# Crossing from one sub-layer to the next: where a row is normalised, who writes its high and low part, and where its transposes stand

## The chip, the cores and the metric

The kernel runs on one core of a Trainium2 chip. The metric is the device time of one launch in microseconds (us). Five engines work side by side, each through its own queue in order: TensorE (PE in the rows, PEld its weight loads), VectorE (DVE), ScalarE (ACT), GpSimd (POOL) and SyncE (SP), which issues most of the DMA transfers.

## The reference, cut to what matters

Two layers of a hybrid backbone over 256 latent and 256 context tokens with 1024 channels. A layer is three sub-layers: a SwiGLU FFN, a mixer of three branches, another FFN. Each takes a modulated input and is followed by a post-norm:

```python
def _ln(x):
    xf = x.astype(jnp.float32)
    mu = jnp.mean(xf, axis=-1, keepdims=True)
    var = jnp.mean(jnp.square(xf - mu), axis=-1, keepdims=True)
    return ((xf - mu) * lax.rsqrt(var + LN_EPS)).astype(x.dtype)

def _post_norm(x, res, g, b):
    return _ln(DN_ALPHA * x + res) * g + b

def _modulate(x, shift, scale):
    return _ln(x) * (1.0 + scale) + shift

# in a layer, for latent tokens (h) and context tokens (hc) alike:
h = _post_norm(h, 0.5 * m[2] * _swiglu(_modulate(h, m[0], m[1]), ...), ...)
y, yc = _mixer(_modulate(h, m[3], m[4]), _modulate(hc, mc[3], mc[4]), ...)
h = _post_norm(h, m[5] * y, ...)
h = _post_norm(h, 0.5 * m[8] * _swiglu(_modulate(h, m[6], m[7]), ...), ...)
```

Between two sub-layers stand two normalisations of the same row: the post-norm of the one and the modulation of the next.

## The kernel before

The 512 tokens are four token tiles of 128 rows (`h`, tokens on partitions); after the second layer's mixer only the two latent tiles go on. Every float32 operand of a matrix product is kept as a high and a low part (type fp32r), and a product is three matmuls, `mm3` (L73): high by high, high by low, low by high. Weights come in chunks (`chunk`, L57): a DMA brings `raw`, ScalarE casts the high part `whi` (L68), VectorE subtracts for the low part `wlo` (L69).

The last step of each sub-layer is a product `pd` with tokens on partitions, tile after tile: in an FFN 11 steps of three matmuls for each half of the columns, 33 products of 512 columns a tile in the last half, in a mixer 24 for each half. When a tile's half is done, `evac` takes it from PSUM into `h` on VectorE (`ev` L259, `h` L262 or L264) and collects statistics (`bst`, `bn` L190). After the second half `boundary` (L268) does the post-norm: aggregate `mv` (L202), the reciprocal root by `nv` on VectorE (L196) and a power on GpSimd (L197), `xn1` on VectorE (L275, the rows show it as `xn`), `h` with its row sum `q` (L276, L280), the sum of squares on ScalarE (L281), and again `nv` and the power. `normed` (L205) multiplies mean and root (`nb`, L210, VectorE) and lets ScalarE write the normalised row `xn` (L211). `modulate` (L214) transposes `xn` on TensorE in eight blocks of 128 x 128 into two PSUM tiles `put` (L222), ScalarE writes the scaled and shifted blocks `uv` (L231), VectorE casts them to the high part `uhi` (L233), and GpSimd subtracts for the low part `ulo` (L234). `uhi` and `ulo` are what the next sub-layer multiplies: its first products are `pg` and `pu` in an FFN (three matmuls each, high by high first) and `pgm` in a mixer.

There are five such seams: FFN to mixer, mixer to FFN, FFN to FFN of the next layer, FFN to mixer, each with four tiles, and mixer to FFN with two. The order of each engine's instructions is made by a scheduler from priorities that follow the order in the program. Tiles 0 and 1 have their `boundary` directly behind their own `evac`. For tiles 2 and 3 it is written after `mark`, and the first products of the next sub-layer, which need only tiles 0 and 1, are put ahead of these by `early`.

Of the kernel before, what the change touches and what calls it, by code (L numbers as in the profile page):

```python
# [8 lines left out]
F32 = mybir.dt.float32  # L9
# [5 lines left out]
D = 1024  # L15
# [11 lines left out]
class Kernel:  # L27
    def __init__(self, tc, ctx, I, out):
# [7 lines left out]
        self.dram = P(name="dram", bufs=1, space=bass.MemoryType.DRAM)  # L36

    def early(self):
        """Ahead of the boundary work of the context tokens."""
        return self.tc.high_priority(offset=self.tc.cur_priority - self.mark)  # L40
# [10 lines left out]
    def side(self, shape, name):  # L51
        """A PSUM tile for work between the matrix products."""
        pool, tag = self.spare
        return pool.tile(shape, F32, name=name, tag=tag)

    # ---------------------------------------------------------------- weights
    def chunk(self, ap, n=2048, pool=None, bufs=None):  # L57
        """[128, n] float32 in DRAM -> list of ([128, 1024] high part, low part)."""
# [14 lines left out]
    def mm3(self, ps, a, b, start, stop):  # L73
        """ps += a^T b, with a, b (high, low) pairs."""
# [30 lines left out]
    def mod_first(self, j, pool):  # L105
        """Shift and scale of model channels 128 j .. 128 j + 127 in the first sub-layer."""
# [22 lines left out]
    def modulate_first(self, j, pool, xn):  # L129
        """u of model channels 128 j .. 128 j + 127, all tokens."""  # L130
# [12 lines left out]
    def mod_out(self, l, n, res):  # L143
        """Adds the bias to columns 512 n .. 512 n + 511; gates go to DRAM as rows."""
# [19 lines left out]
    def mod(self, l, n):  # L164
        """Columns 512 n .. 512 n + 511 of both streams' modulation vectors of layer l, 128 (on partitions) a step."""
# [26 lines left out]
    def rsqrt(self, var, scale):  # L192
        """(var * scale + eps) ** -0.5"""
# [11 lines left out]
    def normed(self, pool, tt, nmu, rs, bufs=2):  # L205
        """(h + nmu) rs of one token tile."""
# [7 lines left out]
    def modulate(self, pool, l, slot, tt, xn, gs=(0, 1), dve=0):  # L214
        """u (feature-major, high and low) = xn (1 + scale) + shift for one token tile."""
        nc = self.nc
        s = TT_S[tt]
        cs = slice(128 * tt, 128 * tt + 128)
        for g in gs:
            pt = self.psd.tile([128, 4, 128], F32, name="put", tag="d")  # L220
            for j in range(4):
                nc.tensor.transpose(pt[:, j], xn[:, 128 * (4 * g + j):128 * (4 * g + j) + 128], self.ident)  # L222
# [1119 lines left out]
```

## Time and profile before

| | before |
|---|---|
| median of 3 runs | 2058.04 us |
| lowest and highest | 2054.61 and 2058.64 us |
| span of the profiled execution | 2059.9 us |
| TensorE busy | 1980.4 us, 96% |
| VectorE busy | 1519.5 us, 74% |
| ScalarE busy | 781.1 us, 38% |
| GpSimd busy | 157.0 us, 8% |

The span is that of one execution, taken with the profiler on. Busy times are sums over it. A matmul's row starts when it enters the array and lasts longer than the distance to the next one, since they are pipelined; how fast they go is read from the distance of two starts. The number in brackets behind a row is how long the engine stood idle before it, and what ended that.

### The profile page before, as it was taken

The numbers are of one execution on the slowest core, as the hardware profiler recorded it, in microseconds if no ns is written. First come the engines' busy times: TensorE is split into PE (matmuls) and PEld (weight loads), VectorE is DVE, ScalarE is ACT, GpSimd is POOL, SyncE is SP. The second block draws the span as 40 slices with busy tenths as digits, with TensorE's granted clock in tenths as the row PEclk, the third lists the DMA queues.
The fourth block names the chain that finished last, engine by engine and source line by source line (L and its number), as shares of the span: only waits on it lengthen the run. The fifth ranks groups of instructions, "written<-read, shape, count | busy, mean of one in ns | idle before, by whom it ended". The sixth has DMA issues, their size and how long they took to land. (4 is left out here: it accounts for less than half of the span.)

```text
span 2059.9 us, 28737 instructions
## 1 busy us (share of the span) xinstructions
PE 1980.4 (96%) x10556; PEld 1644.6 (80%) x10556; DVE 1519.5 (74%) x3352; ACT 781.1 (38%) x1300; POOL 157.0 (8%) x221
## 2 busy tenths in 40 slices
PE   7999999999999999999999989999998999979997
PEld 4888887787767887888888878888887877968896
DVE  4996998868996347766998767768778587684555
ACT  4321332345554224432233252312224566444442
POOL 0000110121100002200000030000003110010000
PEclk9999999999999999999999999999999999998999
DMA  8454566355344333345565525546552643564563
GB/s 312 154 152 143 184 202 215 118 178 163 120 147 133 101 103 123 113 148 180 184 197 186 187 97 188 166 158 198 173 183 88 188 156 117 163 232 136 182 188 112
DMA packets 103119, 333.10 MB, mean 162 GB/s; under 512 B 12353, under 2 KB 25505, under 8 KB 102977
## 3 DMA queue, kind: packets, MB, share of 16 engines
q1 hardware_dynamic: 96384, 310.96, 47.6%
q10 hardware_dynamic: 3584, 14.24, 1.8%
q0 software_dynamic: 3008, 6.07, 1.0%
q8 instruction: 83, 1.36, 0.3%
q14 instruction: 60, 0.48, 0.1%
HBM read 313.70 MB, written 17.51 MB: 161 GB/s over the span
## 5 line engine op out<-in xcount | busy, mean ns | idle before, releaser
L68 ACT CAST whi<-raw 128x1024 fp32r<-128x1024 f32 (+1 forms) x384 | 394.9, 1031 | 615.6 <-PE pd L78 160.2
L69 DVE TENSOR_TENSOR wlo<-raw,whi 128x1024 fp32r<-128x1024 f32 (+1 forms) x384 | 462.7, 1207 | 219.8 <-ACT whi L68 218.3
L178 DVE SCALAR_TENSOR_TENSOR pj<-raw,cb 128x512 f32<-128x512 f32 x512 | 351.7, 706 | 51.3 <-DMA raw<-in_w_modT 47.7
L76 PE MATMUL pg<-uhi,whi 128*128 128x512 f32 (+1 forms) x736 | 265.7, 361 | 1.6 <-DVE uhi L233 1.3
L78 PE MATMUL pg<-uhi,wlo 128*128 128x512 f32 (+1 forms) x736 | 263.1, 357 | 2.3 <-DVE wlo L69 2.3
L76 PE MATMUL pu<-uhi,whi 128*128 128x512 f32 (+1 forms) x736 | 263.2, 358 | 1.5 <-DVE ev L259 1.5
L77 PE MATMUL pg<-ulo,whi 128*128 128x512 f32 (+1 forms) x736 | 263.2, 358 | 0.6 <-POOL ulo L234 0.5
L77 PE MATMUL pu<-ulo,whi 128*128 128x512 f32 (+1 forms) x736 | 262.7, 357 | 0.0
L78 PE MATMUL pu<-uhi,wlo 128*128 128x512 f32 (+1 forms) x736 | 262.5, 357 | 0.0
L77 PE MATMUL pd<-wlo,gT 128*128 128x512 f32 x616 | 240.6, 391 | 1.6 <-DVE wlo L69 1.5
L76 PE MATMUL pd<-whi,gT 128*128 128x512 f32 x616 | 240.8, 391 | 0.9 <-DVE ev L259 0.9
L78 PE MATMUL pd<-whi,gT 128*128 128x512 f32 x616 | 239.5, 390 | 0.0
L76 PEld LDWEIGHTS pg<-uhi,whi 128*128 128x128 f32 x736 | 140.9, 191 | 26.1 <-issue 3.8
L78 PEld LDWEIGHTS pg<-uhi,wlo 128*128 128x128 f32 x736 | 140.7, 191 | 22.0 <-DVE wlo L69 2.7
L76 PEld LDWEIGHTS pu<-uhi,whi 128*128 128x128 f32 x736 | 140.9, 192 | 21.6 <-DVE ev L259 1.7
L77 PEld LDWEIGHTS pg<-ulo,whi 128*128 128x128 f32 x736 | 140.4, 191 | 20.9 <-POOL ulo L234 1.1
L77 PEld LDWEIGHTS pu<-ulo,whi 128*128 128x128 f32 x736 | 140.6, 191 | 20.2 <-issue 0.8
L78 PEld LDWEIGHTS pu<-uhi,wlo 128*128 128x128 f32 x736 | 140.5, 191 | 19.8 <-issue 0.4
L76 PEld LDWEIGHTS pd<-whi,gT 128*128 128x128 f32 x616 | 115.6, 188 | 27.2 <-issue 1.3
L77 PEld LDWEIGHTS pd<-wlo,gT 128*128 128x128 f32 x616 | 115.7, 188 | 25.9 <-DVE wlo L69 2.5
L78 PEld LDWEIGHTS pd<-whi,gT 128*128 128x128 f32 x616 | 115.7, 188 | 23.9
L76 PE MATMUL pgg<-uhi,whi 128*128 128x512 f32 (+1 forms) x384 | 131.8, 344 | 0.0
(561 smaller groups left out, 3234.0 us busy)
## 6 DMA issues: line engine op xcount, KB each, us to landing
raw<-in_w_gu SPq DMA_DIRECT2D x176, 512.0 KB
raw<-in_w_modT SPq DMA_DIRECT2D x128, 512.0 KB
raw<-in_w_dn SPq DMA_DIRECT2D x80, 512.0 KB
raw<-in_w_in SPq DMA_DIRECT2D x80, 512.0 KB
sd<-sst ACTq DMA_DIRECT2D x16, 802.0 KB
sst<-sd SPq DMA_DIRECT2D x16, 802.0 KB
wm<-in_w_mod SPq DMA_DIRECT2D x16, 512.0 KB
raw<-in_w_br SPq DMA_DIRECT2D x16, 512.0 KB
```

What stands on the lines that cost most here:

```text
L68: nc.scalar.copy(hi[:, :m], raw[:, :m])
L69: nc.vector.tensor_sub(lo[:, :m], raw[:, :m], hi[:, :m].bitcast(F32))
L76: mm(ps, a[0], b[0], start=start, stop=False)
L77: mm(ps, a[0], b[1], start=False, stop=False)
L78: mm(ps, a[1], b[0], start=False, stop=stop)
L178: V.scalar_tensor_tensor(junk, raw[:, 512 * k:512 * k + 512], 1.0, self.cb[:, s, 512 * k:512 * k + 512], op0=OP.mult, op1=OP.mult, accum_o ...
```

## The change

`normed`, `modulate`, `early` and `mark` are gone. In their place stands `feed`. It normalises the row on VectorE in one step, (h + nmu) * rs, with no `nb`; after the transposes, ScalarE writes each block's high part `uhi` straight from PSUM, VectorE computes the same block once more from PSUM in float32 (`uv`, eight operations of 128 columns), and VectorE, not GpSimd, subtracts for `ulo`.

`boundary` no longer calls this at once. It leaves it with `later(9.6, ...)`: `mm3` counts down the time of the products that are written after it, and when 9.6 us of them have been written, `feed` is written at that place. The transposes may not be issued ahead of the last matmul written by then (`issue_after`). `flush` writes at once what is left over: after the first half of the first `pg` and `pu` of an FFN, after the first pair of tiles of a mixer, and at the start of an FFN of two tiles. The last `evac`, `boundary` and `feed` are `urgent`, with a raised priority, for all tiles alike. `room` says from which pool and tags `xn` and `uv` take their buffers; in the mixer `uv` takes those of tag "p" (three), which `zs`, the copy that is stored for the state-space branch, uses too. The rest of the diff removes comments.

```diff
     def mm3(self, ps, a, b, start, stop):
         mm = self.nc.tensor.matmul
         mm(ps, a[0], b[0], start=start, stop=False)
         mm(ps, a[0], b[1], start=False, stop=False)
-        mm(ps, a[1], b[0], start=False, stop=stop)
+        self.last = mm(ps, a[1], b[0], start=False, stop=stop)
+        if self.todo:
+            us = 3 * (ps.free_size() + 32) / 2400
+            for x in self.todo:
+                x[0] -= us
+            while self.todo and self.todo[0][0] <= 0:
+                self.todo.pop(0)[1]()
...
+    def urgent(self):
+        return self.tc.high_priority(offset=400)
+    def later(self, us, step):
+        self.todo.append([us, step])
+    def flush(self):
+        todo, self.todo = self.todo, []
+        for _, step in todo:
+            step()
...
-        nc.vector.tensor_mul(nb, nmu, rs)
-        nc.scalar.activation(xn, self.h[:, tt], AF.Identity, bias=nb, scale=rs)
...
-                    nc.scalar.activation(v[:, j], pt[:, j], AF.Identity, bias=sh, scale=sc)
-            ks = slice(4 * g, 4 * g + 4)
-            nc.vector.tensor_copy(self.uhi[:, ks, cs], v)
-            (nc.vector if dve else nc.gpsimd).tensor_sub(self.ulo[:, ks, cs], v, self.uhi[:, ks, cs].bitcast(F32))
+    def feed(self, l, slot, tt, nmu, rs):
+        nc, V = self.nc, self.nc.vector
+        s = TT_S[tt]
+        cs = slice(128 * tt, 128 * tt + 128)
+        pool, xtag, vtag, pp, ptag = self.room
+        with self.urgent():
+            xn = pool.tile([128, D], F32, name="xn", tag=xtag[0], bufs=xtag[1])
+            V.tensor_scalar(xn, self.h[:, tt], nmu, rs, op0=OP.add, op1=OP.mult)
+            for g in range(2):
+                pt = pp.tile([128, 4, 128], F32, name="put", tag=ptag)
+                with self.tc.issue_after(self.last.ins):
+                    for j in range(4):
+                        nc.tensor.transpose(pt[:, j], xn[:, 128 * (4 * g + j):128 * (4 * g + j) + 128], self.ident)
+                v = pool.tile([128, 4, 128], F32, name="uv", tag=vtag[0], bufs=vtag[1])
+                for j in range(4):
+                    k = 4 * g + j
+                    sh = self.modT[l][:, 8 * slot + k, s:s + 1]
+                    sc = self.modT[l][:, 8 * slot + 8 + k, s:s + 1]
+                    nc.scalar.activation(self.uhi[:, k, cs], pt[:, j], AF.Identity, bias=sh, scale=sc)
+                    V.tensor_scalar(v[:, j], pt[:, j], sc, sh, op0=OP.mult, op1=OP.add)
+                ks = slice(4 * g, 4 * g + 4)
+                V.tensor_sub(self.ulo[:, ks, cs], v, self.uhi[:, ks, cs].bitcast(F32))
...
-        self.modulate(pool, *nxt, tt, self.normed(pool, tt, q[:, 1:2], self.rsqrt(q[:, 2:3], 1.0 / D)))
+        rs = self.rsqrt(q[:, 2:3], 1.0 / D)
+        self.later(9.6, lambda: self.feed(*nxt, tt, q[:, 1:2], rs))
...
+            self.room = pool, ("gT", 11), ("sg", 2), self.psd, "d"
+            if len(tiles) < 4:
+                self.flush()
...
-                        with self.early():
-                            W, begun = self.gate_load(l, f, range(2))
-                            self.gate_mm(W, begun, 0, T // 2)
+                        W, begun = self.gate_load(l, f, range(2))
+                        self.gate_mm(W, begun, 0, T // 2)
+                        self.flush()
                         self.gate_mm(W, begun, T // 2, T)
...
+                    self.room = bp, ("xn", 2), ("uv", 2), self.psd, "d"
                     for t in tiles:
                         for k in range(11):
                             step(k, t)
-                        self.evac(pool, nrm, t, ch, ps[t], False, True)
-                        if t < 2:
+                        with self.urgent():
+                            self.evac(pool, nrm, t, ch, ps[t], False, True)
                             self.boundary(bp, nrm, t, nxt)
-                    self.mark = tc.cur_priority
-                    for t in tiles[2:]:
-                        self.boundary(bp, nrm, t, nxt)
...
-                    with self.early():
-                        for _ in moving(ws, (store_z, store_v(0)), (0,)):
-                            pass
+                    self.room = pool, ("PT", 2), ("p", 3), self.psa, "a"
+                    for _ in moving(ws, (store_z, store_v(0)), (0,)):
+                        pass
+                    self.flush()
```

How this moves instructions is seen at the third seam, from the first layer's second FFN (`pd`) to the second layer's first (`pg`, `pu`). On TensorE, before, where `pd` ends:

```order
L78 MATMUL pd<-whi,gT 128x512
L76 MATMUL pg<-uhi,whi 128x256
L77 MATMUL pg<-ulo,whi 128x256
L222 MATMUL put<-ident,xn 128x128 x3
L78 MATMUL pg<-uhi,wlo 128x256
L222 MATMUL put<-ident,xn 128x128
L76 MATMUL pu<-uhi,whi 128x256
L77 MATMUL pu<-ulo,whi 128x256
L78 MATMUL pu<-uhi,wlo 128x256
L76 MATMUL pg<-uhi,whi 128x256
```

After, at the same place:

```order
L89 MATMUL pd<-whi,gT 128x512
L244 MATMUL put<-ident,xn 128x128 x8
L87 MATMUL pd<-whi,gT 128x512
L88 MATMUL pd<-wlo,gT 128x512
L89 MATMUL pd<-whi,gT 128x512
L87 MATMUL pg<-uhi,whi 128x256
L87 MATMUL pu<-uhi,whi 128x256
L87 MATMUL pg<-uhi,whi 128x256
L87 MATMUL pu<-uhi,whi 128x256
L88 MATMUL pg<-ulo,whi 128x256
L89 MATMUL pg<-uhi,wlo 128x256
L88 MATMUL pu<-ulo,whi 128x256
```

Before, the third tile's transposes stood between the first products of the next FFN; now those of the second tile stand three products ahead of the end of `pd`, and high-by-high products come first, then those with `ulo`.

On VectorE at this seam, before, from the aggregate of the third tile on:

```order
L202 BN_AGGR mv<-bst 128x2
L233 CAST uhi<-uv 128x4x128
L196 TENSOR_SCALAR nv<-mv 128x1
L275 SCALAR_TENSOR_TENSOR xn_10494<-h,mv,lng 128x1024
L233 CAST uhi<-uv 128x4x128
L276 SCALAR_TENSOR_TENSOR h,q<-xn_10494,nv,lnb 128x1024
L280 TENSOR_SCALAR q<-q 128x1
L69 TENSOR_TENSOR wlo<-raw,whi 128x1024
L196 TENSOR_SCALAR nv<-q 128x1
L210 TENSOR_TENSOR nb<-q,nv 128x1
L69 TENSOR_TENSOR wlo<-raw,whi 128x1024
L259 TENSOR_TENSOR ev<-pd,gbc_8531 128x512
```

After, from the evacuation of the fourth tile (`ev`) up to the second tile's first `ulo`:

```order
L278 TENSOR_TENSOR ev<-pd,gbc_8563 128x512
L80 TENSOR_TENSOR wlo<-raw,whi 128x1024
L213 TENSOR_SCALAR nv<-q 128x1
L251 TENSOR_SCALAR uv<-put,modT 128x128 x2
L283 TENSOR_TENSOR h<-h,ev 128x512
L251 TENSOR_SCALAR uv<-put,modT 128x128 x2
L207 BN_STATS bst<-h 128x6
L251 TENSOR_SCALAR uv<-put,modT 128x128
L219 BN_AGGR mv<-bst 128x2
L251 TENSOR_SCALAR uv<-put,modT 128x128
L253 TENSOR_TENSOR ulo<-uv,uhi 128x4x128
```

Before, VectorE did two casts per tile for the next sub-layer; now the second tile's eight `uv` stand one by one among the weights' `wlo` and the evacuation of the fourth, and the first `ulo` that the next products need stands behind all of them.

On VectorE at the fifth seam, from mixer to FFN with two tiles, before, from the second tile's last evacuation on:

```order
L259 TENSOR_TENSOR ev<-pd,gbc_16206 128x512
L262 SCALAR_TENSOR_TENSOR h<-h,ev 128x512
L190 BN_STATS bst<-h 128x6
L233 CAST uhi<-uv 128x4x128
L202 BN_AGGR mv<-bst 128x2
L196 TENSOR_SCALAR nv<-mv 128x1
L275 SCALAR_TENSOR_TENSOR xn_16431<-h,mv,lng 128x1024
L233 CAST uhi<-uv 128x4x128
L276 SCALAR_TENSOR_TENSOR h,q<-xn_16431,nv,lnb 128x1024
```

After, from the addition that follows it on:

```order
L281 SCALAR_TENSOR_TENSOR h<-h,ev 128x512
L251 TENSOR_SCALAR uv<-put,modT 128x128
L207 BN_STATS bst<-h 128x6
L251 TENSOR_SCALAR uv<-put,modT 128x128
L219 BN_AGGR mv<-bst 128x2
L251 TENSOR_SCALAR uv<-put,modT 128x128
L213 TENSOR_SCALAR nv<-mv 128x1
L294 SCALAR_TENSOR_TENSOR xn_16499<-h,mv,lng 128x1024
L251 TENSOR_SCALAR uv<-put,modT 128x128
L295 SCALAR_TENSOR_TENSOR h,q<-xn_16499,nv,lnb 128x1024
L251 TENSOR_SCALAR uv<-put,modT 128x128
L299 TENSOR_SCALAR q<-q 128x1
```

Before, two casts of the first tile stood in the chain of the second; now six of the first tile's `uv` do.

## Rows read from the trace of the kernel before

**Rows 1.** The page's part 1: busy time, share of the span, instructions.
```profile
PE 1980.4 (96%) x10556; PEld 1644.6 (80%) x10556; DVE 1519.5 (74%) x3352; ACT 781.1 (38%) x1300; POOL 157.0 (8%) x221
```

**Rows 2.** TensorE's waits: who for whom, us in total, times, longest.
```profile
PE put L222 <- ACT xn L211: 37.8, 18, 10.9
```

**Rows 3.** The five seams' windows: length, busy us by engine, clock, DMA.
```profile
390.00:440.00 50.00, 42.70 (x256) 38.00 (x255) 33.67 (x59) 26.15 (x50) 21.03 (x24) 0.93 0.23 72
795.00:845.00 50.00, 44.47 (x253) 38.73 (x252) 29.43 (x57) 25.19 (x49) 19.87 (x17) 0.97 0.16 48
1180.00:1230.00 50.00, 42.18 (x239) 36.93 (x238) 35.21 (x58) 25.43 (x48) 19.00 (x16) 0.93 0.24 87
1557.00:1607.00 50.00, 42.90 (x259) 37.98 (x258) 32.90 (x56) 25.87 (x49) 20.48 (x24) 0.97 0.33 105
1836.00:1866.00 30.00, 16.50 (x80) 13.90 (x79) 17.96 (x28) 13.81 (x26) 10.06 (x8) 0.72 0.38 130
```

**Rows 4.** TensorE's timeline, first seam: start, us, what, in brackets idle.
```profile
395.06 0.39 PE L78 MATMUL pd<-whi,gT 128*128 128x512 f32 x1
395.28 0.39 PE L76 MATMUL pd<-whi,gT 128*128 128x512 f32 x1
397.02 1.09 PE L222 MATMUL put<-ident,xn 128*128 128x128 f32 x8 [1.35 <-ACT xn L211]
...
418.88 1.76 PE L222 MATMUL put<-ident,xn 128*128 128x128 f32 x7 [4.05 <-ACT xn L211]
```

**Rows 5.** Timeline of the other engines, first seam, its first tile.
```profile
387.71 0.67 DVE L259 TENSOR_TENSOR ev<-pd,gbc 128x512 f32<-128x512 f32 x1
...
390.12 0.15 DVE L196 TENSOR_SCALAR nv<-mv 128x1 f32<-128x1 f32 x1
390.19 1.27 DVE L275 SCALAR_TENSOR_TENSOR xn<-h,mv,lng 128x1024 f32<-128x1024 f32 x1
...
390.36 1.53 POOL L197 TENSOR_TENSOR nv<-nv,mhalf 128x1 f32<-128x1 f32 x1 [44.26 <-DVE nv L196]
...
391.92 1.28 DVE L276 SCALAR_TENSOR_TENSOR h<-xn,nv,lnb 128x1024 f32<-128x1024 f32 x1 [0.46 <-POOL nv L197]
...
393.44 1.15 ACT L281 ACTIVATE xn<-h,q 128x1024 f32<-128x1024 f32 x1 [14.34 <-DVE q L280]
...
395.73 1.24 ACT L211 ACTIVATE xn<-h,nb,nv 128x1024 f32<-128x1024 f32 x1 [1.04 <-DVE nb L210]
```

**Rows 6.** TensorE's timeline: second seam's last tile, third seam's third.
```profile
836.37 1.09 PE L222 MATMUL put<-ident,xn 128*128 128x128 f32 x8 [2.12 <-ACT xn L211]
...
1210.60 0.90 PE L222 MATMUL put<-ident,xn 128*128 128x128 f32 x3 [4.14 <-ACT xn L211]
```

**Rows 7.** Timeline of GpSimd and VectorE, first seam, second and third tile.
```profile
412.23 1.29 POOL L234 TENSOR_TENSOR ulo<-uv,uhi 128x512 fp32r<-128x512 f32 x1
412.29 2.31 DVE L276 SCALAR_TENSOR_TENSOR h<-xn,nv,lnb 128x1024 f32<-128x1024 f32 x1 [0.45 <-POOL nv L197]
```

**Rows 8.** Timeline of TensorE, fifth seam: the second tile's transposes.
```profile
1856.97 1.97 PE L222 MATMUL put<-ident,xn 128*128 128x128 f32 x8 [10.92 <-ACT xn L211]
```

**Rows 9.** Groups by line and shape on VectorE and ScalarE: busy us, mean ns.
```profile
L69 DVE TENSOR_TENSOR wlo<-raw,whi 128x1024 fp32r<-128x1024 f32 x368 | 451.9, 1229 | 214.1 <-ACT whi L68 212.6 <-DMA mt<-kd 0.4
...
L233 DVE CAST uhi<-uv 128x512 fp32r<-128x512 f32 x36 | 20.4, 566 | 36.6 <-ACT uv L231 36.6
...
L141 DVE TENSOR_TENSOR ulo<-uv,uhi 128x512 fp32r<-128x512 f32 x8 | 5.5, 692 | 0.2
...
L633 DVE TENSOR_SCALAR sprm<-sprm,nsg 128x128 f32<-128x128 f32 x16 | 4.6, 285 | 4.6 <-DMA sprm<-in_ssm_bc 4.6
...
L157 DVE TENSOR_SCALAR grw<-pgt 8x128 f32<-8x128 f32 x12 | 3.3, 274 | 7.2 <-PE pgt L155 7.2
...
L781 DVE TENSOR_SCALAR ga<-ga 64x1024 f32<-64x1024 f32 x2 | 1.4, 676 | 0.0
...
L231 ACT ACTIVATE uv<-put,modT 128x128 f32<-128x128 f32 x144 | 52.5, 465 | 19.9 <-PE put L222 19.9
```

More of the change, by code (lines that the diff above doesn't have):

```diff
@@ L36, in __init__ @@
         self.dram = P(name="dram", bufs=1, space=bass.MemoryType.DRAM)
-    def early(self):
-        return self.tc.high_priority(offset=self.tc.cur_priority - self.mark)
+        self.todo = []
+    def urgent(self):
[6 more added lines that the diff above has]
+            step()
     def pool(self, es, name, side="left"):
@@ L212, in normed @@
         return xn
-    def modulate(self, pool, l, slot, tt, xn, gs=(0, 1), dve=0):
-        nc = self.nc
+    def feed(self, l, slot, tt, nmu, rs):
+        nc, V = self.nc, self.nc.vector
         s = TT_S[tt]
         cs = slice(128 * tt, 128 * tt + 128)
[L219 to L222, printed above, removed]
-            v = pool.tile([128, 4, 128], F32, name="uv", tag="uv", bufs=2)
-            for j in range(4):
-                k = 4 * g + j
-                sh = self.modT[l][:, 8 * slot + k, s:s + 1]
-                sc = self.modT[l][:, 8 * slot + 8 + k, s:s + 1]
-                if dve and j >= 4 - dve:
-                    nc.vector.tensor_scalar(v[:, j], pt[:, j], sc, sh, op0=OP.mult, op1=OP.add)
-                else:
-                    nc.scalar.activation(v[:, j], pt[:, j], AF.Identity, bias=sh, scale=sc)
-            ks = slice(4 * g, 4 * g + 4)
-            nc.vector.tensor_copy(self.uhi[:, ks, cs], v)
-            (nc.vector if dve else nc.gpsimd).tensor_sub(self.ulo[:, ks, cs], v, self.uhi[:, ks, cs].bitcast(F32))
@@ L1101, in mixer @@
                     self.psum(e2, d=3, o=2)
+                    self.room = pool, ("xn", 2), ("uv", 2), self.psd, "d"
                     w = [[x for i in range(2) for x in self.chunk(I["w_out"][l, ch, i], 2048, *((pool, 4) if ch else ()))] for ch in range(2)]
@@ L1111, in mixer @@
                                          (hi[:, o:o + 512], lo[:, o:o + 512]), start=k == 0, stop=k == 7)
-                            self.evac(pool, nrm, t, ch, ps, True, True)
-                        if t < 2:
+                            with self.urgent():
+                                self.evac(pool, nrm, t, ch, ps, True, True)
+                        with self.urgent():
                             self.boundary(pool, nrm, t, nxt)
-                    self.mark = self.tc.cur_priority
-                    for t in tiles[2:]:
-                        self.boundary(pool, nrm, t, nxt)
     def merge(self, l, pool, ys, yT, T, stationary, mo, ths):
```

## The prediction

> **What bounds the kernel now.** TensorE: the page has it busy for 96% of the span, VectorE for 74% [rows 1]. What TensorE can still win lies where it stands, so the list of its waits comes next: the transposes `put` wait for ScalarE's normalised row `xn`, 37.8 us in 18 waits, one for each token tile that crosses one of the five seams [rows 2]. The windows give each seam its idle time (length less PE busy) and the mean granted clock [rows 3]: 7.3, 5.5, 7.8, 7.1 and 13.5 us idle, in order; and the clock, 0.93, 0.97, 0.93, 0.97 and 0.72 of 2.4 GHz, costs 50 x 0.07 = 3.5, then 1.5, 3.5, 1.5 and 30 x 0.28 = 8.4 us (each figure uncertain by 0.2 from rounding). Together some 41 + 18 = 59 us of 2059.9 are at stake; where the longest wait was 2.1 us the clock took 1.5, where it was 4.1 it took 3.5 [rows 4, 6].
>
> Then the chain of one tile at the first seam [rows 5]: `xn1` 1.27, GpSimd's power 1.53, `h` 1.28, Square from 393.44, another power, ScalarE's `xn` 1.24, and the transposes at 397.02, after 1.35 us idle [rows 4]. VectorE stands idle in it, for 0.46 us ahead of `h`, then behind Square and behind the second power [rows 5]: before, the chain is bound by hand-overs, not by VectorE. From the second tile on the two engines also get into each other's way: `h` takes 2.31 us where it begins together with GpSimd's `ulo` [rows 7], 1.28 where it is alone [rows 5].
>
> **The change, part by part.**
> *Prices.* The new row normalisation on VectorE is a two-scalar operation over 1024 columns; the row of that form has 0.676 us, on 64 partitions [rows 9]. The bounds are 0.68 and 1.27 (the two-tensor `xn1` [rows 5]); I take 0.68, the same form. `uv`, 128 columns out of PSUM: nearest are 0.285 (128 columns, SBUF) and 0.274 (PSUM, 8 partitions) [rows 9]; I take 0.28, and 0.21 to 0.36 for the range. `ulo` on VectorE is 0.69 [rows 9]. An operation that needs nothing from the one ahead starts about 0.08 before that one's duration is over (`nv` lasts 0.15, `xn1` starts 0.07 after it [rows 5]): so `uv` counts at 0.20, `ulo` and `xn` at 0.61.
> *VectorE's account.* A tile loses `nb` (0.08) and two casts (mean 0.566 [rows 9], swollen by GpSimd; I take 0.4 each); it gains `xn` 0.6, eight `uv` 1.6 and two `ulo` 1.2. So net 2.5 us more per tile. With the rest of the tile's work from [rows 5] (2.5 from the second half's `ev` to `xn1`; `xn1` 1.2; `h` 1.3; `q`, `nv` 0.2) VectorE has 8.6 us a tile. A tile's matrix work is 33 products at 0.22 to 0.23 [rows 4], 7.5 us, and the weights' `wlo`, 1.2 each [rows 9], come on top. So through a seam VectorE falls behind, where before it had gaps. This is what I think decides.
> *GpSimd* loses its 36 `ulo`, and with them the doubled `h` and `xn1`: worth up to 1 us a tile on the chain [rows 5, 7].
> *ScalarE* loses `xn`; its eight writes per tile stay at 0.465 [rows 9]. But now ScalarE and VectorE read the same `put` tile, and the built program keeps them apart: each `uv` waits for ScalarE's write of that block, and the next write in the tile waits for that `uv`. Four rounds of 0.465 + 0.28 + two hand-overs of 0.05 to 0.1 (`nv` ends 390.27, the power starts 390.36 [rows 5]) are 3.4 to 3.8 us for the two `put` tiles side by side, where eight writes alone take 8 x 0.36 = 2.9. No row of the kernel before shows two engines reading one `put`. The Trainium skill, "PSUM — Partial Sum Buffer", section "PSUM bank collisions raise a hardware error", says that two engines must not access one bank in the same 32 partitions at once, two reads included: a rule against sharing `put`, and by it the rounds are needed. Were they not, each seam's last tile would be ready 0.5 us sooner and the sum 2.5 us lower.
> *Placement.* At the first seam the first tile's transposes go from 37 products behind the tile's end to 53, and the second's from 34 to 63. `xn` of the first now stands behind the next tile's evacuation, statistics and `xn1` on VectorE: 394.8 (the tile's end, four products ahead of the old place, plus 0.4) + 2.5 + 1.2 + 0.7 = 399.2, against a place at 395.5 + 16 x 0.2275 = 399.15. So 0.1 to 0.4 of waiting is left of 1.35, and nothing of the second's; at the other three seams of four tiles it is much the same. What is late next is not `xn` but what stands on VectorE behind it.
> *First and fourth seam* (mixer next). From the third tile's end to `ulo` of the second, VectorE has in a row: the third's evacuation and statistics with four `uv` and the first tile's `ulo` between, 4.0; `xn1`, `xn`, `h` 3.1; two `wlo` 2.3; the fourth's evacuation and statistics 2.3; nine `uv` 1.8 and `ulo` 0.6: some 14.2 us. TensorE has 7.5 of `pd`, 0.9 of transposes, and 3 of mixer products that need no `ulo` of that tile: it waits about 3 (1.9 for the bank that `ev` of the fourth frees, then 1.3). Behind follow two more `wlo` with the fourth's `xn1` and `h` between, 2.1, and the `put` bank that the alternation holds and the third's `ulo`, 2.2. With 0.5 for the rest 8.2 idle against 7.3, but no wait over 2 us, so clock loss 1 instead of 3.5: **-1.6**. At the fourth the clock lost only 1.5 before: 8.0 against 7.1 and 1 against 1.5, **+0.4**.
> *Second seam* (mixer to FFN): the first two tiles' waits and that of a first product for `ev` go; 0.6 for a transpose, 2.0 for a `wlo` that stands behind the fourth tile's chain, 2.2 for its `ulo` come: 4.8 against 5.5, the same clock, **-0.7**.
> *Third seam* (FFN to FFN). The 14.2 us are the same (second order excerpt), but only four first products lie before the first that needs `ulo`: 14.2 - 7.5 - 0.9 = about 5.6 of waiting where 4.14 stood [rows 6], 2.1 for the fourth tile's `ulo`, 0.6 else: 8.3 to 8.7 against 7.8, the same clock, **+0.7**.
> *Fifth seam* (two tiles, nothing between). The transposes stay right behind the last `pd`. Of the 10.92 [rows 8] GpSimd's interference (about 2) and ScalarE's `xn` against VectorE's (0.7) go; six `uv` now stand within the chain, each able to hold it for the write that it waits for (1 to 2 in all): 9.5 to 10.6. Behind the transposes the first `ulo` comes after four rounds and 0.7 where before the casts were ready after half: 1.5 later. Together **+0.2**, between -1.5 and +1.5.
> Sum: -1.6 - 0.7 + 0.7 + 0.4 + 0.2 = -1.0; I take **-1.5**, since GpSimd's relief also speeds the aggregate chain of each third tile, which I have counted at bare durations only in part. From 2059.9 that is 2058.4. The profiled execution lies 1.9 above the median of the three runs, 2058.04 (the three spread over 4 us), so against the runs **2056.5**.
>
> **Rivals.**
> *The waits go as meant.* If VectorE keeps up (`uv` at 0.2, hand-overs hidden), the `put` waits of the four big seams, 37.8 - 10.9 = 26.9, and half their 10 us of clock go, less 5 to 10 left for `wlo` and `ulo`: 20 to 26 gained, 2032 to 2038. For it: VectorE was idle in the chain [rows 5]. Against: 8.6 us a tile on 7.5. A half-way case, `uv` 0.21, gives 8 x 0.07 = 0.6 us a tile on the bound, twice or three times a seam: another 6 to 8, 2049 to 2051.
> *Slower: VectorE becomes the bound for longer than the seam.* The place is the `ulo` of second and fourth tile; the price is what `uv` and `xn` cost above my rows. At `uv` 0.36 and `xn` 1.27 a tile has 1.2 us more; two tiles of each seam carry it, 2.4 x 4, plus 1 at the fifth: +10, 2067. At the mixer seams `uv` of the last tile also takes a buffer that the store of `z` has to leave first, 0 to 4 us. It decides from about +0.35 us a tile (0.04 on each `uv`).
> *It does not do what it says.* 9.6 us are 42 products, and the scheduler put 53 and 63: the fixed stretch is not what sets the place, and the fifth seam has no stretch at all. That leaves the sums above as they are.
>
> **How the numbers follow.** About 0.2%, 4 us, is what can be told from no change here. The forecast, within 4 us of before: 0.45. Half-way or better: 0.23 for 2045 to 2054, 0.13 for the waits going. Slower by over 4: 0.19, mostly up to 2067. The likeliest's own range is 2054 to 2062; for 8 in 10 I leave out the far end of the full gain and of the loss: 2044 to 2067. Faster 0.36, same 0.45, slower 0.19.
>
> **What would show it.** `put` waits of the four big seams fall from some 26 to under 4; waits of `pg` and `pgm` for `ulo` and `wlo` rise from almost nothing to 15 to 20. VectorE's busy time rises by 18 x 2.5 = 45 us, less some 20 for contention. `h` and `xn1` stay at 1.3 with no 2.3. The last `put` wait stays near 10. Wrong, if TensorE shows no wait for `ulo`; if `uv` is far from 0.28; or if the `put` waits stay.

## The result, and the profile after

| | before | after |
|---|---|---|
| median | 2058.34 us | 2076.51 us |
| lowest and highest | 2054.61 and 2059.45 us | 2071.45 and 2083.84 us |
| span of the profiled execution | 2059.9 us | 2079.0 us |

The ratio of after to before is 1.0097, 95% interval 1.0080 to 1.0114: 20 us slower. The forecast was 2056.5 with a range up to 2067, so it was wrong, on the side of its second rival.

The page's part 1 of after, against [rows 1]: VectorE has 46.8 us more, GpSimd 48.9 less, TensorE 8.9 more for the same 10556 matmuls.

```profile
PE 1989.3 (96%) x10556; PEld 1652.5 (79%) x10556; DVE 1566.3 (75%) x3496; ACT 765.8 (37%) x1282; POOL 108.1 (5%) x185
```

TensorE's waits in after, with who was waited for, us in total, times, longest:

```profile
PE pg L88 <- DVE ulo L253: 14.2, 4, 4.5
PE put L244 <- DVE xn L239: 11.7, 3, 10.8
PE pgm L89 <- DVE ulo L253: 9.1, 4, 5.4
...
PE pd L88 <- DVE wlo L80: 5.3, 5, 2.2
PE pg L89 <- DVE wlo L80: 4.5, 2, 2.4
...
PE psu L776 <- ACT Zs L771: 4.0, 2, 3.8
```

The same waits for `ulo` and `wlo` in before:

```profile
PE pd L77 <- DVE wlo L69: 3.4, 4, 1.5
PE pg L78 <- DVE wlo L69: 2.3, 1, 2.3
...
PE pg L77 <- POOL ulo L234: 0.5, 1, 0.5
```

The waits for `xn` have gone from 37.8 [rows 2] to 11.7, of which 10.8 is the last seam's. In their place stand 23.3 us for `ulo`, where 0.5 stood; those for `wlo` have gone from 5.7 to 9.8. All of them wait for VectorE. The row was moved out of TensorE's way, and the low parts were moved into it.

The groups on VectorE and ScalarE that answer to [rows 5, 9] (busy us, mean ns of one, idle before and what ended it):

```profile
L251 DVE TENSOR_SCALAR uv<-put,modT 128x128 f32<-128x128 f32 x144 | 55.3, 404 | 19.7 <-ACT uhi L250 11.0 <-DMA zt<-zs 8.3
L295 DVE SCALAR_TENSOR_TENSOR h<-xn,nv,lnb 128x1024 f32<-128x1024 f32 x20 | 25.7, 1284 | 3.9 <-POOL nv L214 3.1
...
L253 DVE TENSOR_TENSOR ulo<-uv,uhi 128x512 fp32r<-128x512 f32 x36 | 24.9, 707 | 0.2
L239 DVE TENSOR_SCALAR xn<-h,q,nv 128x1024 f32<-128x1024 f32 x18 | 14.5, 808 | 1.6 <-POOL nv L214 1.5
...
L250 ACT ACTIVATE uhi<-put,modT 128x128 fp32r<-128x128 f32 x144 | 60.6, 456 | 89.8 <-PE put L244 50.5 <-DVE uv L251 37.3
```

`h` is back at its undisturbed 1.28, as forecast. `uv` is not at 0.28 but at 0.404, outside the range given for it; 8.3 us of its waiting is for a transfer, the store of `z`; and ScalarE stands 37.3 us behind `uv`.

Whole seams, 100 us each and 50 for the last, before and then after (length, busy us of TensorE, weight loads, VectorE, ScalarE, GpSimd, then the granted clock as a mean, 1 being 2.4 GHz):

```profile
380.00:480.00 100.00, 90.69 (x544) 78.54 (x543) 72.44 (x138) 42.58 (x79) 23.56 (x32) 0.97 0.43 134
785.00:885.00 100.00, 94.47 (x513) 81.83 (x512) 75.63 (x150) 40.81 (x67) 23.03 (x21) 0.98 0.36 116
1170.00:1270.00 100.00, 92.18 (x497) 79.87 (x497) 77.44 (x143) 39.83 (x66) 19.00 (x16) 0.97 0.39 127
1555.00:1655.00 100.00, 91.51 (x613) 80.30 (x614) 69.30 (x128) 52.84 (x104) 27.18 (x40) 0.98 0.45 140
1830.00:1880.00 50.00, 35.74 (x216) 31.86 (x216) 31.26 (x46) 23.05 (x38) 10.09 (x8) 0.83 0.49 165
```

```profile
380.00:480.00 100.00, 87.87 (x507) 76.06 (x506) 78.03 (x161) 38.05 (x74) 12.58 (x22) 0.95 0.40 126
785.00:885.00 100.00, 91.15 (x486) 79.11 (x486) 86.68 (x180) 35.77 (x60) 11.96 (x13) 0.95 0.33 109
1170.00:1270.00 100.00, 91.41 (x488) 79.66 (x488) 82.24 (x168) 35.22 (x62) 8.13 (x8) 0.95 0.36 117
1555.00:1655.00 100.00, 87.94 (x528) 77.53 (x527) 73.80 (x142) 38.95 (x76) 12.88 (x22) 0.93 0.38 118
1843.00:1893.00 50.00, 35.04 (x191) 30.34 (x190) 37.66 (x63) 22.81 (x35) 5.04 (x4) 0.83 0.52 179
```

TensorE is idle for 2.8, 3.3, 0.8, 3.6 and 0.7 us more in these stretches, 11.2 together, and the clock, lower by 0.02, 0.03, 0.02 and 0.05, costs 2, 3, 2 and 5 us more, 12 together. The two sets don't hold quite the same work. So the seams are also told by one matrix product at a time: the n-th product into a tile of a name is the same work in both traces, and the difference of its start times tells how much a kernel is behind. What each seam adds to that difference, with the products that start at 387, 600, 1000, 1400, 1750 and 2040 us in before (one profiled execution of each kernel, so some 2 us of uncertainty in each):

| us added against before | seam 1 | seam 2 | seam 3 | seam 4 | seam 5 |
|---|---|---|---|---|---|
| predicted | -1.6 | -0.7 | +0.7 | +0.4 | +0.2 |
| after | +1.8 | +6.0 | +2.0 | +12.2 | -1.0 |
| e1, store of z apart | -3.8 | +4.1 | +1.9 | -1.1 | +0.3 |
| e3b, the same, eight writes on ScalarE with a cast | -7.7 | -1.5 | -7.4 | -0.6 | -3.5 |
| e8, before with `ulo` on VectorE | -8.3 | -3.2 | -5.6 | -3.0 | -1.3 |
| e15, VectorE's load without rounds | -2.2 | +7.0 | -2.1 | +1.9 | -2.0 |
| e18, rounds with a smaller load | -4.5 | +6.4 | +4.0 | +6.6 | +0.4 |

The worst seam is the fourth, the mixer's. VectorE's timeline there in after, then the store's issue on ScalarE's queue and TensorE's wait (start, us, what, idle before):

```profile
1606.64 0.69 DVE L1072 COPY v<-pgm 128x512 f32<-128x512 f32 x1 [0.52 <-PE pgm L89]
...
1608.86 1.70 DVE L253 TENSOR_TENSOR ulo<-uv,uhi 128x512 fp32r<-128x512 f32 x2
1613.57 0.73 DVE L251 TENSOR_SCALAR uv<-put,modT 128x128 f32<-128x128 f32 x2 [3.01 <-DMA zt<-zs]
1614.51 0.76 DVE L251 TENSOR_SCALAR uv<-put,modT 128x128 f32<-128x128 f32 x2 [0.21 <-ACT uhi L250]
...
1616.38 0.76 DVE L251 TENSOR_SCALAR uv<-put,modT 128x128 f32<-128x128 f32 x2 [0.18 <-ACT uhi L250]
1617.06 1.28 DVE L253 TENSOR_TENSOR ulo<-uv,uhi 128x512 fp32r<-128x512 f32 x2
```

```profile
1606.22 0.39 ACTq L1069 DMA_DIRECT2D zt<-zs  x1
```

```profile
1617.80 0.58 PE L89 MATMUL pgm<-whi,ulo 128*128 128x256 f32 x1 [3.15 <-DVE ulo L253]
```

The buffer that the last tile's `uv` needs holds `zs`, the copy of z on its way to DRAM. Its store is issued at 1606.22 and lets go at 1613.57, 7.35 us later; VectorE, which executes in order, stands for 3.01 us, and with it `ulo` and TensorE. At the first seam it is the same with 9.1 us (428.20 to 437.34), 5.27 of standing and 5.41 on TensorE. The rounds (ScalarE and VectorE taking turns on a block of `put`) are visible too: 1613.57, 1614.51, and so on to 1616.38, one each 0.937 us, four in 3.75; that part was forecast at 3.4 to 3.8.

The second seam has another. Rows of VectorE in after, with TensorE's wait below:

```profile
838.81 0.81 DVE L239 TENSOR_SCALAR xn<-h,q,nv 128x1024 f32<-128x1024 f32 x1
...
841.20 0.85 DVE L251 TENSOR_SCALAR uv<-put,modT 128x128 f32<-128x128 f32 x2 [1.51 <-ACT uhi L250]
843.81 0.28 DVE L654 TENSOR_SCALAR sprm<-sprm,nsg 128x128 f32<-128x128 f32 x1 [1.76 <-DMA nsg<-in_nsgn]
844.01 0.72 DVE L251 TENSOR_SCALAR uv<-put,modT 128x128 f32<-128x128 f32 x2
...
846.56 1.28 DVE L253 TENSOR_TENSOR ulo<-uv,uhi 128x512 fp32r<-128x512 f32 x2
```

```profile
847.29 0.58 PE L88 MATMUL pg<-ulo,whi 128*128 128x256 f32 x1 [4.04 <-DVE ulo L253]
```

Between the first and the second round VectorE meets an operation of the state-space side stream that waits 1.76 us for a load. In before the eight writes were ScalarE's and such an operation could hold up only the casts behind them; now it stands inside the chain. Ahead of it the first round had waited 1.51 us for ScalarE.

### The profile page after: what moved, and what is told of

Read it like the earlier page. It is cut to its first block, busy times and chain, and to the rows that moved or that the text cites. A ratio compares the mean times of both kernels' runs of the same rounds, so it can differ in the third digit from the quotient of the medians.

```text
span 2079.0 us, 28768 instructions
## 1 busy us (share of the span) xinstructions
PE 1989.3 (96%) x10556; PEld 1652.5 (79%) x10556; DVE 1566.3 (75%) x3496; ACT 765.8 (37%) x1282; POOL 108.1 (5%) x185
## 4 chain that ended last, share of the span: by engine, by line
PE 57%; DVE 9%; issue 3%; DMA 3%; ACT 2%; POOL 1%; SPq 0%; POOLq 0%; ACTq 0%; DVEq 0%
PE pg L88 5%; PE pg L87 5%; PE pg L89 5%; PE pu L89 5%; PE pu L88 5%; PE pu L87 5%; PE pd L88 4%; PE pd L87 4%; PE pd L89 4%; PE pgg L87 3%; PE pgg L89 3%; PE pgg L88 3%; DVE wlo L80 1%; DMA sst<-sd 1%; DVE uv L251 1%
## 5 line engine op out<-in xcount | busy, mean ns | idle before, releaser
L88 PE MATMUL pg<-ulo,whi 128*128 128x512 f32 (+1 forms) x736 | 263.9, 359 | 14.2 <-DVE ulo L253 14.2
L87 PEld LDWEIGHTS pd<-whi,gT 128*128 128x128 f32 x616 | 115.6, 188 | 25.5 <-issue 0.6
```

What stands on the lines that cost most here:

```text
L87: mm(ps, a[0], b[0], start=start, stop=False)
L88: mm(ps, a[0], b[1], start=False, stop=False)
```

## The experiments

All ratios are to before, measured beside it; a difference in us is that of two ratios (before has 1) times 2058. The change has four parts: the row on VectorE (R), the direct high part with eight `uv` on VectorE (D), `ulo` on VectorE instead of GpSimd (U), and the placement (P), which is the later place and the raised priority together; no run parts these two.

**e1_zs_apart.** The changed kernel, z copied to a place that `uv` doesn't use:

```diff
-  z = pool.tile([128, 2, 256], F32, name="zs", tag="p", bufs=3)
+  z = yS[:, tp].rearrange("p (t c) -> p t c", t=2)
```

> The changed kernel with one edit: the copy of z that is stored at the start of each mixer lies in yS, which nothing uses yet, and no longer in the buffers of tag p that uv takes too. Theory store: in the two mixer seams the last tile's uv waits 5.3 and 3.0 us for that store to land, TensorE 5.4 and 3.2 behind it, and the slow clock and late weights behind these cost as much again; then both waits go and the time falls by 9 to 16 us, to 2061 to 2068. Theory load: VectorE has too much work in every seam and the store only hides it; then uv starts sooner but wlo and ulo stay late and the time falls by less than 5 us.

2061.77 us, 1.0019 [1.0008, 1.0031]: 16 us of the changed kernel's 20 hang on that buffer. The table shows where: seams 1 and 4, the mixer's, lose 5.6 and 13.3 less. TensorE's `pgm` waits for `ulo` fall from 9.1 to 0.6 and those of `psu` for `Zs` from 4.0 to 1.0. The windows of the first and the fourth seam, as above, show the clock at 0.98 in both, where after has 0.95 and 0.93:

```profile
380.00:480.00 100.00, 93.83 (x561) 80.76 (x559) 83.44 (x174) 41.89 (x84) 13.85 (x25) 0.98 0.46 143
...
1555.00:1655.00 100.00, 93.31 (x619) 81.01 (x618) 78.60 (x160) 48.94 (x101) 17.79 (x32) 0.98 0.44 141
```

What is left is TensorE's wait for `ulo` in the FFNs, as long as in after:

```profile
PE pg L88 <- DVE ulo L253: 14.0, 4, 4.5
```

**e2_pool_ulo.** The changed kernel without U.

```diff
-  V.tensor_sub(self.ulo[:, ks, cs], v, self.uhi[:, ks, cs].bitcast(F32))
+  nc.gpsimd.tensor_sub(self.ulo[:, ks, cs], v, self.uhi[:, ks, cs].bitcast(F32))
```

> The changed kernel with ulo back on GpSimd. Theory load by count: VectorE loses 2 x 0.6 us a tile, the waits for ulo fall by 1 to 2 us each and the time falls by 5 to 10. Theory contention: GpSimd's 1.3 us per half and the doubled h and xn beside it cost more than VectorE gains, the time stays or rises by up to 8.

2081.97 us, 1.0117 [1.0097, 1.0138], 4 us more than the changed kernel, with overlapping intervals. U is worth 20 us alone (e8, below), 26 beside R (e5 to e9) and 26 beside P (e7 to e13; all below), but nothing that can be told here, where D is in as well. That points to D as the part that eats it; e6 below shows the same without R and P.

**e3_cast.** The changed kernel without D: ScalarE writes `uv`, VectorE casts four blocks at once.

```diff
-  nc.scalar.activation(self.uhi[:, k, cs], pt[:, j], AF.Identity, bias=sh, scale=sc)
-  V.tensor_scalar(v[:, j], pt[:, j], sc, sh, op0=OP.mult, op1=OP.add)
+  nc.scalar.activation(v[:, j], pt[:, j], AF.Identity, bias=sh, scale=sc)
...
+  V.tensor_copy(self.uhi[:, ks, cs], v)
```

> The changed kernel with the high part by the old way: ScalarE writes uv from PSUM, VectorE casts uhi in two instructions of 512 columns; row on VectorE, ulo on VectorE and the placement stay. Theory load: the eight uv of 0.40 us (3.2 us a tile, less overlap 2.6) and the rounds between the two engines on one put tile are what makes VectorE late; a tile loses 2.6 and gains 0.7, no wait for ulo over 2 us is left and the time falls below the kernel before, to 2035 to 2050. Theory store: uv is written by ScalarE into the same buffers, which still wait for the store, so the waits of 5.4 and 3.2 at the mixer seams stay and the time is 2062 or more.

2038.09 us, 0.9893 [0.9871, 0.9916]: without D the change gains 22 us. Three of TensorE's waits in it, for `xn`, `wlo` and `ulo`:

```profile
PE put L244 <- DVE xn L239: 12.8, 5, 9.6
...
PE pd L88 <- DVE wlo L80: 6.0, 6, 2.2
...
PE pg L88 <- DVE ulo L253: 1.2, 2, 0.8
```

The waits for the row stay away, and no wait for `ulo` over 0.8 us takes their place.

**e4_xn_act.** The changed kernel without R (`nb` on VectorE, `xn` on ScalarE as before).

```diff
-  V.tensor_scalar(xn, self.h[:, tt], nmu, rs, op0=OP.add, op1=OP.mult)
...
+  V.tensor_mul(nb, nmu, rs)
+  nc.scalar.activation(xn, self.h[:, tt], AF.Identity, bias=nb, scale=rs)
```

> The changed kernel with the normalised row back on ScalarE (nb on VectorE). If the 0.8 us of the row on VectorE matter for the queue behind it, the time falls by 2 to 5 us; if the chain of the fifth seam (10.8 us of waiting, where the hand-over to ScalarE and its 1.24 come back) and ScalarE's own queue matter more, it rises by 1 to 5.

2072.56 us, 1.0068 [1.0047, 1.0088]: next to the changed kernel, with overlapping intervals.

**e8_before_ulo.** The kernel before with U alone:

```diff
-  (nc.vector if dve else nc.gpsimd).tensor_sub(self.ulo[:, ks, cs], v, self.uhi[:, ks, cs].bitcast(F32))
+  nc.vector.tensor_sub(self.ulo[:, ks, cs], v, self.uhi[:, ks, cs].bitcast(F32))
```

> The kernel before with one edit: the low part ulo is subtracted by VectorE, not by GpSimd. Theory contention: GpSimd's 1.3 us halves double h, xn1 and the casts beside them (2.3 for 1.3 us) and sit in front of the powers, so 1.3 us a tile on VectorE is cheaper than what they cost: h stays at 1.28, the put waits shrink by 1 to 2 us for each tile after the first, the time falls by 8 to 20 us, to 2038 to 2050. Theory load: any work added to VectorE at the seams makes it later, the time rises by 2 to 10.

2038.08 us, 0.9903 [0.9888, 0.9918]: one operation moved gives 20 us. TensorE's wait for the row, and VectorE's groups:

```profile
PE put L222 <- ACT xn L211: 25.5, 17, 9.9
```

```profile
L276 DVE SCALAR_TENSOR_TENSOR h<-xn,nv,lnb 128x1024 f32<-128x1024 f32 x20 | 25.7, 1283 | 4.3 <-POOL nv L197 3.6
...
L233 DVE CAST uhi<-uv 128x512 fp32r<-128x512 f32 x36 | 15.2, 422 | 28.6 <-ACT uv L231 28.4
```

`put` waits fall by 12.3 from 37.8 [rows 2], the cast by 0.144 from 0.566 [rows 9], and `h`, which had a mean of 1.715 before, is always as in its undisturbed row [rows 5]. All seams gain. `h`, `xn1` and the casts together took 15.7 us less of VectorE, 0.87 a tile. `ulo` has also left GpSimd's queue, in which the powers stand; this run doesn't part the two.

**e5_before_xn** (before with R alone), **e6_before_hi** (before with D and U), **e9_before_xn_ulo** (before with R and U). In e5 and e9 the edit is

```diff
-  nc.vector.tensor_mul(nb, nmu, rs)
-  nc.scalar.activation(xn, self.h[:, tt], AF.Identity, bias=nb, scale=rs)
+  nc.vector.tensor_scalar(xn, self.h[:, tt], nmu, rs, op0=OP.add, op1=OP.mult)
```

and in e6, beside `ulo` as in e8,

```diff
-  nc.scalar.activation(v[:, j], pt[:, j], AF.Identity, bias=sh, scale=sc)
+  nc.scalar.activation(self.uhi[:, k, cs], pt[:, j], AF.Identity, bias=sh, scale=sc)
+  nc.vector.tensor_scalar(v[:, j], pt[:, j], sc, sh, op0=OP.mult, op1=OP.add)
...
-  nc.vector.tensor_copy(self.uhi[:, ks, cs], v)
```

> The kernel before with one edit: the row is normalised by VectorE in one step. If the hand-over and ScalarE's 1.24 us are what the put waits are made of, each of the 18 waits falls by 0.5 to 1 us and the time by 8 to 15. If the step stands behind other work in VectorE's queue (the next tile's evacuation, weights) and shares the engine with GpSimd's ulo, what is won is lost again or more: the time stays or rises, by up to 12.

> The kernel before with one edit: the high part straight from the transposes, uv once more on VectorE in eight operations and ulo on VectorE; row and placement as before. Theory load: the eight uv and the rounds cost more than the two casts, so against the variant that only moves ulo to VectorE it is 15 to 25 us slower, about 2055 to 2065. Theory placement: the parts are harmless and the placement with raised priority is what costs; then it is as fast as the variant that only moves ulo.

> The kernel before with two edits: row on VectorE in one step, and ulo on VectorE. The row alone was 18 us slower, ulo alone 20 us faster. If the row's step lost only because it stood next to GpSimd's ulo (contention), it wins here: 2028 to 2036. If it loses by its place in VectorE's queue, behind the next tile's evacuation, the loss stays: 2042 to 2056.

e5 2076.19 us, 1.0081 [1.0062, 1.0099]; e6 2056.94 us, 0.9995 [0.9985, 1.0005]; e9 2048.74 us, 0.9953 [0.9941, 0.9966]. In the old place the row on VectorE costs 17 us alone, more than the 12 allowed for, and 10 beside U (e9 against e8). In e5 the transposes wait for it as long as they did for ScalarE's (36.4 us), so nothing is won; why it costs that much isn't shown. The waits don't tell it, as those of e9 are shorter than the 25.5 of e8:

```profile
PE put L220 <- DVE xn L209: 20.6, 13, 10.5
```

The edit in `normed` also takes in the four rows at the kernel's start, which stay on ScalarE in the changed kernel. Told by the n-th product as above, e9 is already some 3 us (uncertain by 2) behind e8 at 387 us, ahead of the first seam, so the edit is a little more than R. D beside U costs 19 (e6 against e8): it takes all of U's gain.

**e7_place_only** (before with P alone) and **e13_cast_xn_act** (P and U). Both are the changed kernel with the edits of e3 and e4; e7 has that of e2 as well.

> Placement and priorities of the changed kernel alone: row on ScalarE, high part by a cast, ulo on GpSimd, as in the kernel before. If the later place hides the put waits, which were 37.8 us, as the change means it to, the time falls by 10 to 25 us. If the waits move on to the first products that need ulo and wlo, it stays within 5 us of the kernel before.

> Placement and priorities of the changed kernel and ulo on VectorE, but the row on ScalarE and the high part by a cast: against the kernel before, placement and ulo alone. If the placement is what a row on VectorE needs and gives nothing else, this is as fast as ulo alone, 2036 to 2042. If placing the transposes later wins by itself, 2025 to 2034; if the changed order costs, 2043 or more.

e7 2067.67 us, 1.0046 [1.0034, 1.0058]; e13 2042.0 us, 0.9919 [0.9893, 0.9944]. P alone loses 9.5 us, where a gain or no more than 5 us had been expected; beside U it changes nothing that can be told (e13 against e8). Beside R and U it gains 12 (e3 against e9). In these pairs P is worth something only with the row on VectorE; and with P the row costs nothing (e13 to e3, 5.4 us faster, with overlapping intervals).

**e10_one_reader** and **e11_cast_actcast.** Both with z apart and the cast to `uhi` on ScalarE, out of `uv`; in e10 the eight `uv` are VectorE's, in e11 ScalarE's. No `put` tile has two readers in either, so they differ by who writes `uv`: by VectorE's load, ScalarE's, and a hand-over from VectorE to the cast.

```diff
-  nc.scalar.activation(self.uhi[:, k, cs], pt[:, j], AF.Identity, bias=sh, scale=sc)
...
+  nc.scalar.copy(self.uhi[:, ks, cs], v)
```

> The changed kernel with the store of z out of the way, and the high part cast by ScalarE from uv in SBUF, two casts of 512 columns in place of its eight writes from PSUM. VectorE has the same eight uv and two ulo as in the changed kernel, but only one engine reads put. Theory rounds: waiting for each other on put is what makes the 18 tiles late, so it falls from 2062 to 2045 to 2056. Theory load: VectorE's own 0.40 us per uv and its place in the queue are the cost, and the cast comes on top of the chain; then it stays at 2058 to 2066.

> The variant with row and ulo on VectorE, high part by a cast and the new placement (2038 us), with the cast on ScalarE in place of VectorE, and the store of z in yS. If VectorE's load is still what is late in the seams, 0.7 us a tile less there gives 3 to 8 us: 2030 to 2035. If ScalarE's queue, where the cast now stands between uv and the weights, is late instead, as the variant with one reader suggests, 2040 or more.

e10 2069.15 us, 1.0054 [1.0039, 1.0069], above both expectations; e11 2042.58 us, 0.9924 [0.9901, 0.9948]. Taking the rounds away at the same load (e10 against e1) made it 7 us slower; the likely reason, not tested by itself, is that ScalarE's cast, 0.616 us, now stands behind all of a group's `uv` (8.1 us of `pg` waits for `uhi`). The two against each other: 27 us for 50.9 us of `uv` on VectorE, 0.53 for each:

```profile
L250 DVE TENSOR_SCALAR uv<-put,modT 128x128 f32<-128x128 f32 x144 | 50.9, 403 | 6.3 <-PE put L244 6.3
```

**e15_load, e17_rounds, e3b_cast_zs, e18_rounds_zs** tell VectorE's load and the rounds apart. e3b is e3 with z apart; e15 and e17 are built on e3, e18 on e3b. e15 adds eight operations a tile that touch no PSUM and that nobody needs; e17 and e18 add eight that read one column of each block of `put`, so that ScalarE and VectorE take turns. Their outcome isn't used.

```diff
   nc.scalar.activation(v[:, j], pt[:, j], AF.Identity, bias=sh, scale=sc)
+  V.tensor_scalar(jk, xn[:, 512 * (k // 4):512 * (k // 4) + 256], sc, sh, op0=OP.mult, op1=OP.add)
```

That is e15; in e17 and e18 the added line is

```diff
+  V.tensor_scalar(jk, pt[:, j, 0:1], sc, sh, op0=OP.mult, op1=OP.add)
```

> The version with the eight writes on ScalarE, the cast on VectorE and the rest of the change (2038.1), plus eight scaling operations a tile of 256 columns out of the row xn on VectorE, between the eight writes; they read no PSUM and nobody reads what they write. So VectorE gets some 2.5 us a tile more, about what the eight of the changed kernel cost it (3.2, less two casts of 0.4), but no bank is shared between the engines. If VectorE's load is what the direct high part costs: 2055 to 2065, with waits of TensorE for ulo and wlo of 10 us or more. If the rounds on the shared bank are: 2037 to 2045.

> The same version (2038.1), plus eight operations a tile on VectorE that read one column of the block of put that ScalarE has just written out: the rounds (a write of ScalarE, a read by VectorE, the next write) are those of the changed kernel, while VectorE gets at most some 1.5 us a tile more, by the shortest operations in the trace. If the rounds cost it: 2052 to 2065. If VectorE's load does: 2039 to 2048, in proportion to what the eight come to in the trace.

> The same version (2038.1) with the copy of z that goes to DRAM taken out of the row's half of yS instead of a buffer that uv also uses. With the eight writes on ScalarE and VectorE keeping up, little waits for that store any more: 2033 to 2039 by the load theory; were the store's wait a price of its own, as behind the changed kernel (14.7 us), 2023 to 2030.

> The forced rounds of the run before (2084.6), now on the version whose z copy has room of its own (2035.3), so that no write of uv waits for the store. The eight reads of one column took 0.276 us each there, 39.5 us of VectorE in all, against 59.5 for the eight loads that cost 26.4. Were load the only price: 2035.3 + 26.4 x 39.5 / 59.5 = 2053. If the rounds have a price of their own and the store's was some 15: 2066 to 2073.

e3b 2035.32 us, 0.9896 [0.9879, 0.9913]; e15 2064.44 us, 1.0039 [1.0025, 1.0054]; e17 2084.63 us, 1.0131 [1.0114, 1.0148]; e18 2075.33 us, 1.0093 [1.0070, 1.0116]. The added operations in e15, and TensorE's waits:

```profile
L252 DVE TENSOR_SCALAR jk<-xn,modT 128x256 f32<-128x256 f32 x144 | 59.5, 413 | 1.8
```

```profile
PE pgm L88 <- DVE q L301: 12.8, 2, 6.4
...
PE pd L88 <- DVE wlo L80: 7.7, 5, 3.3
PE pg L89 <- DVE wlo L80: 6.7, 3, 3.2
PE pg L87 <- DVE uhi L254: 5.7, 3, 2.3
```

Load alone, put into the seams, brings waits for VectorE back and costs 30 us against e3 for 59.5 us of operations, 0.50 us for each; e10 against e11 gave 0.53. By the intervals each rate is uncertain by 0.1. In e18, ScalarE's and VectorE's groups:

```profile
L250 ACT ACTIVATE uv<-put,modT 128x128 f32<-128x128 f32 x144 | 64.4, 457 | 93.9 <-DVE jk L252 53.8 <-PE put L244 39.6 <-DVE ulo L255 0.4
L252 DVE TENSOR_SCALAR jk<-put,modT 128x1 f32<-128x1 f32 x144 | 39.6, 275 | 24.6 <-ACT uv L250 24.6
```

By load alone e18 would be 39.6 x 0.50 to 0.53 = 20 to 21 us above e3b; it is 40.5 above. So rounds have a price of their own: some 20 us, uncertain by 7, where the two engines wait 78.4 us for each other. e18 lies above what was expected for it and e17 far above both of its theories: load and rounds both cost, where each theory had one of them. In e17 `uv`, now ScalarE's, also stood 8.7 us behind the store of z; against e18 that is 8 us. In e3 against e3b the store costs nothing that can be told, and no wait for it appears in e3.

## Why the prediction was wrong

The runs give the change as a chain in which one part is added at a time:

| step | us |
|---|---|
| before to e8: `ulo` off GpSimd | -20.0 |
| e8 to e9: the row on VectorE | +10.3 |
| e9 to e3: the placement | -12.3 |
| e3 to after: the direct high part | +42.0 |
| sum | +20.0 |

The price of a part depends on what is already there. By another order, e8 to e13 to e3, the placement comes at +3.3 and the row at -5.4, neither of which can be told from nothing.

The last step, by e1, e3 and e3b: 16.1 for the store of z, 25.3 for the rest, 0.6 between e3 and e3b, which is nothing that can be told. Of the 25.3, VectorE's net load (55.3 of `uv` less 36 casts at 0.42 us, 40.2) accounts for 20 to 21 at the rates above; that leaves 4 to 5 for the rounds, while e18's rate, scaled by the waiting (39.7 us of the two engines for each other in e1, 78.4 in e18), would give 10. With each rate uncertain by 0.1, what the rounds cost here may be anything from nothing to 10; the runs don't settle it more finely.

By the prediction's own steps:

- **The price of `uv`: wrong.** 0.28 was taken, with 0.21 to 0.36 for the range; it is 0.404. The nearest rows [rows 9] were 128 columns in SBUF and 8 partitions in PSUM; neither was both wide and from PSUM, and the upper end was set too near to them. `xn` is 0.81, not 0.68. Counted as the prediction counts (0.08 off each), the account has 0.32 x 8 + 0.73 instead of 2.2 a tile, 1.1 us more: 9.7 on 7.5.
- **The account as what decides: right in kind.** The rival "VectorE becomes the bound" said that this decides from 0.35 us a tile and gave 2067 for 1.2 more. e3 and e15 bear it out: with the load gone the waits for `ulo` go, with another load put in its place VectorE is waited for again. Without the store the result would have lain within the range, at 2061.8 (e1). That this is near the forecast is in part luck: U alone gains 20 us and D beside it loses 19 (e6), and the sum had neither at that size.
- **The store of z: this is the term that put the time out of the range.** It was seen, in the rival, and priced at 0 to 4 us; the forecast's own sum names nothing for it; it took 16. What was missed was its landing time, 7.35 and 9.1 us, and that VectorE's standing is passed on: 8.3 us of it became 8.6 on TensorE (5.41 and 3.15), and the clock was 0.95 and 0.93 in the two windows where e1 has 0.98 in both. So the first and the fourth seam, forecast at -1.6 and +0.4, came at +1.8 and +12.2; without the store they are at -3.8 and -1.1.
- **Second seam: sign wrong.** -0.7 was forecast, +6.0 came, +4.1 in e1 (no store of z lies in this seam; the two can't be told apart by this table). The waits for `wlo` (2.1) and `ulo` were named, but `ulo` took 4.04 instead of 2.2. In the chain ahead of it VectorE stands 1.76 us for the side stream's operation, which the working left out, as it left out that the clock falls (0.98 to 0.95, 3 us).
- **Third and fifth seams: nearly right.** +0.7 was forecast and +2.0 came; +0.2 and -1.0. The last `put` wait is 10.78, its forecast some 10.
- **GpSimd's relief: right in size, but not in the sum.** "Up to 1 us a tile" was given, and e8 shows 0.87 a tile on VectorE and 20 us of time. The sum has it only in that the new chains are counted at bare durations, and 0.5 us beside that. With it, and without D, the rival "the waits go as meant", 2032 to 2038, is reached: e3 comes to 2038.1, with the `put` waits of the big seams down to 3.2 us and those for `ulo` to 1.2.
- **What would show it.** The `put` waits for `xn` in the four big seams (0.9), the last one (10.8) and `h` at 1.28 came as listed. The waits of `pg` and `pgm` for `ulo` and `wlo` came at 27.8, above the 15 to 20 listed, and VectorE's busy time rose by 46.8, where 45 less 20 had been listed. The mark for being wrong came too, a `uv` far from 0.28.
- **Slips in the sums.** The first seam's VectorE row adds up to 14.1, not 14.2, and its idle time to 8.0, not 8.2; the third seam's wait is 5.8 by its own terms, not 5.6. None of this matters beside the store.

The rounds were forecast at 3.4 to 3.8 us for a tile and are 3.75 at the last tile of both mixer seams. The Trainium skill, "PSUM — Partial Sum Buffer", section "PSUM bank collisions raise a hardware error", says that two engines must not access one bank in the same 32 partitions at once, two reads included. No run here lets them, so what it would bring stays open; e3 avoids the question by having one reader.

Six versions beat both kernels: e3, e3b, e8, e11, e13 and, behind them, e9 (0.9953). All six leave out D. The best three, e3, e3b and e8, can't be told apart (0.9893, 0.9896 and 0.9903), so the one-line edit of e8 is as good as any.

## What to carry over

Measure a change's parts alone: here one of four was worth 20 us alone and another lost 42 beside the rest, and the sum hid both. In these seams, operations put into VectorE's part of the chain cost about half their duration in time (e15, and e10 against e11), so a step "saved" on the way (a cast) must be weighed against all that the saving issues there. That is no rule for every move: `ulo` went to VectorE as well and gained 20 us by what it took away from GpSimd. Before a tile takes a buffer that a store has to leave, read from a trace how long such a store takes to land; here VectorE, which works in order, passed the whole of that wait on to TensorE.

## What was not expected of the hardware

- VectorE's two-scalar operation out of PSUM: one column on 128 partitions took 0.275 us (e18), 128 columns 0.404 (after). By these two, some 0.27 is there for one column already, and each further one adds 1.0 ns. From SBUF, 128 columns took 0.285 [rows 9] and 256 columns 0.413 (e15).
- 36 subtractions on GpSimd (1.47 us each in the mean), in an engine that is busy for 8% of the span, cost 20 us against the same on VectorE (0.69 each, e8). Without them `h` took 8.6 us less in all (20 x 0.432) and the casts 5.2 (36 x 0.144).
- A store of 256 KB that was issued on ScalarE's queue let go of its buffer 7.35 to 9.1 us later.
